# A hybrid decoder block on one core: the recurrence at 8.25 products a half instead of 8.5, gate loads behind operand loads, and another order of the first rows

## The chip, the cores and the metric

The kernel runs on one core of a Trainium2 chip. TensorE (PE) multiplies matrices into PSUM, VectorE (DVE) and ScalarE (ACT) do elementwise work, GpSimd (POOL) does small work and issues the transfers that add to memory, and SyncE (SP) issues most other transfers. Each of these takes its instructions in order, so an instruction that waits holds all that is queued behind it on its engine. The metric is the device time of one launch in microseconds (us), lower is better. The median of three runs before the change is 1466.38 us.

## The reference

One layer of a decoder block on x (1024 tokens x 1024 columns), float32:

```python
proj = x @ w_in                       # 1024 x 7168: q | f | i | o_gate | pool_v | gate_a | gate_b
qf = silu(q) * 128 ** -0.5
f = lb + (1 - lb) * sigmoid(f_pre); k = 1 - f
# 8 heads of 128: S_t = diag(f_t) S_{t-1} + k_t i_t^T,  o_t = S_t^T q_t
o = o * rsqrt(mean(o * o, per head) + RMS_EPS) * hgrn_norm_g * sigmoid(o_gate)
a = o @ w_a
pooled = causal_mean(pool_v, windows 2, 4, 8, 16 by group) - pool_v
b = (pooled, group by group, @ w_pool) * pool_scale
merged = sigmoid(gate_a) * a + sigmoid(gate_b) * b
x = layer_norm(2 ** 0.25 * x + merged @ w_out)
x = layer_norm(2 ** 0.25 * x + relu(x @ w_up) ** 2 @ w_down)
```

## The kernel before

**Products.** A float32 operand is split in a high part (a cast on ACT, L126 for weights, L131 for activations) and a low part (a subtract on DVE, L127 and L132). A product of a 512-row weight block with 512 tokens is 12 matmuls of 128x512: for each of four quarters of the contraction, high x high (L212), high x low (L214) and low x high (L215). The function `pair` computes four 512-token by 128-column blocks, each a sum of two such block products, with seven products instead of eight, in the manner of Strassen and Winograd: the weight blocks b11, b12, b21, b22 and their combinations T1 to T4 against the activation combinations a11, a12, a22, s1 to s4. An ordinary pair takes its operands in the order T0 (b11), b21, T2, T3, T1, T4, b22; a `twin` pair, in the w_a stage, in the order T0, b21, T3, T4, T2, T1, b22. T3 = b22 - b12 (L284) needs the last block loaded. Weight blocks live in a ring of six (`raw`), of which a pair takes five, so the loads of the next pair wait until combinations of this one have been split.

**Stages.** To about 97 us: x is transposed on PE (L170), split, and the value projection i is computed (L501 to L503). From 97 to 668 us: 24 pairs of w_in, for the heads' q and f (`head_inputs`), the output gates (`output_gates`), the pooled columns (`pooled`) and the gates a and b (`gates`). Then w_a in two runs of two pairs, w_out with the first norm, the MLP's up and down products, and the last norm at 1465.

**The recurrence** is a generator that runs beside the pairs of w_in: after each product PE takes one step of it (a "turn"). Its 16 halves (8 heads x 512 tokens) take `PER_HALF` = 8.5 products each, rounded; at a half's fourth turn the half before is put out (`turn_outputs`, L1034 multiplies by the output gate in the buffer `og`, and `put_output` stores it and adds it to up to three of the sums s1 to s4 in memory, by transfers on POOL, L640). The last half's output comes at turn 149, the second product of gates(6). ORDER is the list of pairs. Behind it come gates(6) and gates(7), with the 16 pooled products of w_pool (`pool_products`, L113 to L115) spread behind their products by `POOL_AFTER`. The weight parts of a pooled group lie in a ring of the tiles tD, tE, tF and og.

**Who sets the order.** From the first output gates to gates(7) PE's order is that of the code. On the other engines, a scheduler orders the instructions by priorities and estimated times; `issue_after` holds an instruction behind another.

**The w_a stage.** `o_operand` loads the recurrence's output and its sums (tiles c, L618) and splits them into a11, a12, s3, a22, s2, s1, s4, in this order, one ahead of each step. `gated` loads a gate a (tile ga) and the pooled result (tile gb) at the point at which a result block is ready, multiplies (L1120) and adds (L1121). The loads of both kinds are SP's.

Of the kernel before, what the change touches and what calls it, by code (L numbers as in the profile page):

```python
# [12 lines left out]
AF = mybir.ActivationFunctionType  # L13
# [13 lines left out]
HALO = 16  # L27
LINE = 16
NW = 10
PER_HALF = 8.5  # L30
TURN_BACK = 4
TURNS_AHEAD = 3
ORDER = (
    ("inputs", 1), ("pooled", 0), ("inputs", 2), ("gates", 0), ("output_gates", 2), ("inputs", 3), ("pooled", 1),
    ("inputs", 4), ("output_gates", 4), ("gates", 1), ("inputs", 5), ("pooled", 2), ("inputs", 6), ("output_gates", 6),
    ("gates", 2), ("inputs", 7), ("pooled", 3), ("gates", 3), ("gates", 4), ("gates", 5),
)
POOL_AFTER = {6: (1, 1, 1, 1, 1, 1, 2), 7: (2, 2, 2, 2, 0, 0, 0)}
PRIO_WHOLE = 6000
QUARTER = HALF // 2  # L40
PRIO = 60
# [10 lines left out]
def tile_hybrid_block(  # L52
# [18 lines left out]
    nc = tc.nc  # L71
# [83 lines left out]
    r = [None] * 8  # L155
    xp = {name: [None] * CH for name in ("a11", "a12", "a22", "s1", "s2", "s3", "s4")}

    made_last, made_hi = {}, {}

    @contextmanager  # L160
    def behind_parts(name):
# [10 lines left out]

    def in_parts(name, kp, src):
        xp[name][kp] = act_tile()
        made_last[name], made_hi[name] = (i.ins for i in split_into(xp[name][kp], src))


    xt = [[None] * CH for _ in range(3)]
# [88 lines left out]
    def pair(raw, rooms, takes, pz_tag="pj", twin=False, pc_tag="pj", turned=False):  # L267


        b11, b12, b21, b22, t = raw if len(raw) == 5 else (*raw, None)  # L270
        c, ps = {}, {}

        def copied(room, ps):
            t = room()
            A.copy(t, ps)  # L275
            return t

        def added(t, ps):
            V.tensor_add(t, t, ps)  # L279
            return t  # L280

        def make_t3():
            c["t"] = block_tile() if t is None else t
            V.tensor_sub(c["t"], b22, b12)  # L284

        def t3():
            if twin:
                make_t3()
            return w_part(c["t"])

        def t2():
            if not twin:
                make_t3()
                make_t2()
            return w_part(b11)

        def make_t2():
            if turned:
                minus_sum(b11, c["t"], b11)
            else:  # L300
                V.tensor_add(b11, c["t"], b11)

        def t4():
            if twin:
                make_t2()
            if turned:
                minus_sum(b21, b11, b21)
            else:
                V.tensor_sub(b21, b21, b11)
            return w_part(b21)  # L310

        def t1():
            if turned:
                minus_sum(b12, b22, b11)
            else:
                V.tensor_sub(b12, b22, b11)
            return w_part(b12)

        def p1(w):
            ps["a"] = ps_tile()  # L320
            prod(ps["a"], w, "a11", True)
            c[11] = copied(rooms[0], ps["a"])

        def p2(w):
            if pz_tag == "pj":
                ps["z"] = ps_tile()
# [97 lines left out]
    with tc.tile_pool(name="xr", bufs=8, side="right", reuse_waits="tile") as xr:  # L424
# [15 lines left out]
        V.tensor_max(lb, prm[:, 0:8], prm[:, 8:16])  # L440
        V.tensor_sub(e01[:, 0:8], prm[:, 0:8], lb)
        V.tensor_sub(e01[:, 8:16], prm[:, 8:16], lb)
        A.activation(e01, e01, AF.Exp)
        V.tensor_add(lb, e01[:, 0:8], e01[:, 8:16])
        V.reciprocal(lb, lb)
        V.tensor_mul(lb, lb, e01[:, 0:8])
        V.tensor_scalar(one_lb, lb, -1.0, 1.0, ALU.mult, ALU.add)
        g_neg = e01[:, 0:8]
        V.tensor_scalar_mul(g_neg, g_col, -1.0)
        x_rows = [xr.tile([P, CH, D], F32, name=f"x{u}", bufs=1) for u in range(2)]  # L450
        for t in range(8):
            r[t] = x_rows[t // CH][:, t % CH]
# [103 lines left out]
            put(0, 1, c, t)  # L556

        first_tokens("a11", "tr", "tr", "hg", "hg")
        w = parts(b11)
        first_tokens("a12", "tr")  # L560
        onto_chain(w, "a11", True, copied(c11, c_late))
        with behind_parts("a11"):
# [53 lines left out]
    def loaded(src, tile_of):  # L616
        t = tile_of()
        nc.sync.dma_start(out=t, in_=src)  # L618
        return t

    def o_operand(name):

        where = dict(a11=lambda kp: od[kp][0], a12=lambda kp: od[kp + CH][0], a22=lambda kp: od[kp + CH][1])
        for kp in range(CH):
            src = where[name](kp) if name in where else osd[name][kp]
            xp[name][kp] = act_tile()
            split_into(xp[name][kp], loaded(src, c_tile))
# [17 lines left out]
    with tc.tile_pool(name="tmp", bufs=1, side="right", reuse_waits="tile") as tmp:  # L645
# [470 lines left out]
        def gated(j, u, park):  # L1116

            def take(src):
                t = loaded(gad[j][u], mg_tile("ga", 12))
                V.tensor_mul(t, t, src)  # L1120
                V.tensor_add(t, t, loaded(pbd[j][u], mg_tile("gb", 2)))  # L1121
                if park:
                    parked[u, j] = t
                else:
                    merged[u][j] = split_act(t)
            return take
# [403 lines left out]
```

## Time and profile before

| | |
|---|---|
| median of 3 runs | 1466.38 us (1464.82 to 1467.86) |
| profiled execution | 1466.59 us |
| its span | 1464.9 us |
| around the span | 1.7 us |
| busy: PE / DVE / ACT / POOL | 1435.5 / 1100.1 / 759.0 / 107.6 us |
| 110 to 600 us (w_in pairs with the recurrence): PE busy | 484.0 of 490 us |
| 600 to 640 us (end of gates(5), gates(6)): PE busy, DMA share | 37.0 of 40 us, 0.87 |
| 640 to 668 us (gates(7)): PE busy, DMA share | 27.5 of 28 us, 0.84 |
| 668 to 720 us (first w_a pairs): PE busy, DMA share | 48.5 of 52 us, 0.73 |

The span is the profiled time from the first to the last recorded instruction. Busy time is a sum over one engine's instructions with overlaps counted once. In a row of a timeline stand the start, the duration, the engine, the line of the code, the operation, the tiles (written <- read) and the shape; what stands in brackets is the idle time of the engine before the instruction and what ended it. A "q" behind an engine's name is its queue of transfers: such a row shows the issue, not the transfer. PEclk, the granted clock, is the share of full speed at which PE may run in a stretch.

### The profile page before, as it was taken

The page shows a single profiled execution, that of the slowest core. Times are in us where ns is not written, and L with a number is a line of the kernel's source. Part 1 is how long each engine was busy: PE and PEld are TensorE (multiplying, and loading weights), DVE is VectorE, ACT ScalarE, POOL GpSimd, SP SyncE. Part 2 cuts the span into 40 slices and gives each one's busy share as a digit, 9 for nine tenths or more (in the row PEclk, how much of TensorE's full clock was granted, in tenths as well). Part 3 has the DMA queues.
Part 4 walks back from the last instruction along what each step waited for, and adds up shares of the span by engine and source line. Part 5 has one row for each costly group of instructions (what it writes and reads, how often), then busy time and mean ns, then how long its engine had stood idle before and what let it go on. Part 6 is the DMA issues. An engine that isn't in the chain of part 4 may idle for free.

```text
span 1464.9 us, 20840 instructions
## 1 busy us (share of the span) xinstructions
PE 1435.5 (98%) x7377; PEld 1188.4 (81%) x7377; DVE 1100.1 (75%) x1807; ACT 759.0 (52%) x1383; POOL 107.6 (7%) x288
## 2 busy tenths in 40 slices
PE   8999999999999999999999999999999999999997
PEld 7788888788878888877788878888888888888886
DVE  4967886796797796477985598666666787777977
ACT  5545566655755655555542366555556443333435
POOL 0002011211211210000002100000000100000000
PEclk9999999999999999999999999999999999999999
DMA  7142245345435546788673135444447774445422
GB/s 259 58 137 87 73 126 169 80 134 155 109 87 146 142 116 184 211 300 286 204 232 113 61 99 180 144 154 148 157 148 261 280 262 142 166 132 170 129 72 115
DMA packets 187161, 228.15 MB, mean 156 GB/s; under 512 B 12176, under 2 KB 110512, under 8 KB 187056
## 3 DMA queue, kind: packets, MB, share of 16 engines
q1 hardware_dynamic: 181088, 212.91, 43.9%
q0 software_dynamic: 5184, 11.54, 4.0%
q10 hardware_dynamic: 784, 2.38, 0.5%
q8 instruction: 58, 0.95, 0.3%
q14 instruction: 47, 0.39, 0.1%
HBM read 149.70 MB, written 77.07 MB: 155 GB/s over the span
## 4 chain that ended last, share of the span: by engine, by line
PE 87%; DVE 6%; DMA 4%; issue 1%; ACT 1%; SPq 0%; DVEq 0%; POOL 0%; ACTq 0%
PE ps_pj L212 15%; PE ps_pj L215 14%; PE ps_pj L214 14%; PE ps_pj L1412 4%; PE ps_pj L1413 4%; PE ps_pj L1411 4%; PE ps_pj L114 2%; PE ps_pj L113 2%; PE ps_pj L115 2%; PE ps_tr L1412 1%; PE ps_tr L1413 1%; PE ps_tr L1411 1%; PE ps_sc L215 1%; DVE w L127 1%; PE ps_hg L215 1%
## 5 line engine op out<-in xcount | busy, mean ns | idle before, releaser
L212 PE MATMUL ps_pj<-act,w 128*128 128x512 f32 x1068 | 420.2, 395 | 10.8 <-ACT c L275 3.3
L215 PE MATMUL ps_pj<-act,w 128*128 128x512 f32 x1068 | 415.7, 391 | 1.3 <-DVE w L127 1.3
L214 PE MATMUL ps_pj<-act,w 128*128 128x512 f32 x1068 | 415.0, 390 | 0.0
L126 ACT CAST w<-raw 128x512 fp32r<-128x512 f32 x310 | 192.5, 622 | 278.1 <-PE ps_pj L214 201.7
L127 DVE TENSOR_TENSOR w<-raw,w 128x512 fp32r<-128x512 f32 x310 | 212.1, 686 | 92.8 <-ACT w L126 87.6
L212 PEld LDWEIGHTS ps_pj<-act,w 128*128 128x128 f32 x1068 | 200.7, 188 | 56.9 <-ACT c L275 4.6
L215 PEld LDWEIGHTS ps_pj<-act,w 128*128 128x128 f32 x1068 | 200.8, 188 | 45.2 <-DVE w L127 2.6
L214 PEld LDWEIGHTS ps_pj<-act,w 128*128 128x128 f32 x1068 | 200.8, 188 | 40.8 <-DVE act L132 0.2
L1373 ACT CAST act<-act 128x1024 fp32r<-128x1024 f32 x66 | 66.9, 1050 | 109.0 <-issue 35.0
L279 DVE TENSOR_TENSOR c<-c,ps_pj 128x512 f32<-128x512 f32 x95 | 64.8, 682 | 39.1 <-PE ps_pj L215 35.6
L1374 DVE TENSOR_TENSOR act<-act,act 128x1024 fp32r<-128x1024 f32 x66 | 79.5, 1220 | 18.5 <-ACT act L1373 17.4
L1413 PE MATMUL ps_pj<-act,act 128*128 128x512 f32 x240 | 93.0, 389 | 0.0
L1412 PE MATMUL ps_pj<-act,act 128*128 128x512 f32 x240 | 93.0, 389 | 0.0
L1411 PE MATMUL ps_pj<-act,act 128*128 128x512 f32 x240 | 92.5, 389 | 0.0
L275 ACT COPY c<-ps_pj 128x512 f32<-128x512 f32 x96 | 55.8, 581 | 3.1 <-issue 1.8
L284 DVE TENSOR_TENSOR raw<-raw,raw 128x512 f32<-128x512 f32 x43 | 29.6, 690 | 33.2 <-DMA raw<-in_w_in_dram 28.8
L1411 PEld LDWEIGHTS ps_pj<-act,act 128*128 128x128 f32 x240 | 45.0, 188 | 9.4
L1412 PEld LDWEIGHTS ps_pj<-act,act 128*128 128x128 f32 x240 | 45.0, 188 | 9.4
L1413 PEld LDWEIGHTS ps_pj<-act,act 128*128 128x128 f32 x240 | 45.0, 188 | 9.3
L1282 ACT ACTIVATE c<-c 128x512 f32<-128x512 f32 x61 | 38.5, 632 | 1.7
L1281 ACT ACTIVATE c<-c 128x512 f32<-128x512 f32 x46 | 29.1, 632 | 15.0 <-DVE c L279 15.0
L1367 DVE TENSOR_TENSOR act<-act,ps_pj 128x512 f32<-128x512 f32 x45 | 30.1, 682 | 6.0 <-PE ps_pj L1413 5.7
(416 smaller groups left out, 2680.5 us busy)
## 6 DMA issues: line engine op xcount, KB each, us to landing
h<-c SPq DMA_DIRECT2D x106, 256.0 KB, 2.7
raw<-in_w_in_dram SPq DMA_DIRECT2D x100, 256.0 KB, 3.3
act<-h SPq DMA_DIRECT2D x78, 256.0 KB, 3.0
draw<-in_w_down_dram SPq DMA_DIRECT2D x16, 1024.0 KB, 7.6
raw<-in_w_up_dram SPq DMA_DIRECT2D x56, 256.0 KB, 2.8
hf<-h SPq DMA_DIRECT2D x34, 256.0 KB, 3.0
s<-og POOLq DMA_DIRECT2D x28, 256.0 KB, 6.1
v<-v SPq DMA_DIRECT2D x16, 256.0 KB, 3.3
```

The source lines that it names most:

```text
L126: A.copy(hi, src)
L127: V.tensor_sub(lo, src, f(hi))
L212: PE.matmul(ps, wh[:, k], th, start=first and k == 0, stop=False, skip_group_check=True)
L214: PE.matmul(ps, wh[:, k], tl, start=False, stop=False, skip_group_check=True)
L215: PE.matmul(ps, wl[:, k], th, start=False, stop=k == CH - 1, skip_group_check=True)
L275: A.copy(t, ps)
L279: V.tensor_add(t, t, ps)
L1373: A.copy(hi, src)
L1374: V.tensor_sub(lo, src, f(hi))
L1411: PE.matmul(ps, hh[:, w], wh, start=fresh and n == 0, stop=False, skip_group_check=True)
L1412: PE.matmul(ps, hh[:, w], wl, start=False, stop=False, skip_group_check=True)
L1413: PE.matmul(ps, hl[:, w], wh, start=False, stop=n == M - 1, skip_group_check=True)
```

## The change

- PER_HALF goes from 8.5 to 8.25. With the rounding, the 17 rounds take 140 products behind the first turns instead of 144, and the last half is put out at turn 145, the fifth product of gates(5), instead of turn 149.
- In ORDER inputs(7) stands ahead of gates(2).
- POOL_AFTER for gates(6) is (0, 1, 1, 1, 1, 2, 2) instead of (1, 1, 1, 1, 1, 1, 2): eight pooled products as before, the first one product later.
- In `pair` T2 is written over b12 instead of b11, and T1 into the tile t (that held T3) instead of b12. T4 is made from b12.
- At the start the third and fourth row of b11 are split behind the first tokens' second and fourth parts, and the small operations for lb and the norm gain stand behind the first tokens.
- In the w_a stage the loads of gate a and of the pooled result are held behind the last load of an operand issued so far in the code, and stand together. All three copies of a pair go into the ring `room`, now of 6; `ga` has 10 buffers instead of 12.

```diff
-PER_HALF = 8.5
+PER_HALF = 8.25
...
-    ("gates", 2), ("inputs", 7), ("pooled", 3), ("gates", 3), ("gates", 4), ("gates", 5),
+    ("inputs", 7), ("gates", 2), ("pooled", 3), ("gates", 3), ("gates", 4), ("gates", 5),
 )
-POOL_AFTER = {6: (1, 1, 1, 1, 1, 1, 2), 7: (2, 2, 2, 2, 0, 0, 0)}
+POOL_AFTER = {6: (0, 1, 1, 1, 1, 2, 2), 7: (2, 2, 2, 2, 0, 0, 0)}
...
-        made_last[name], made_hi[name] = (i.ins for i in split_into(xp[name][kp], src))
+        made_last[name], made_hi[name] = made_kp[name, kp] = [i.ins for i in split_into(xp[name][kp], src)]
...
-            return w_part(b11)
+            return w_part(b12)
 
         def make_t2():
             if turned:
-                minus_sum(b11, c["t"], b11)
+                minus_sum(b12, c["t"], b11)
             else:
-                V.tensor_add(b11, c["t"], b11)
+                V.tensor_add(b12, c["t"], b11)
...
-                V.tensor_sub(b21, b21, b11)
+                V.tensor_sub(b21, b21, b12)
...
-                V.tensor_sub(b12, b22, b11)
-            return w_part(b12)
+                V.tensor_sub(c["t"], b22, b12)
+            return w_part(c["t"])
...
-        w = parts(b11)
+        w = parts(b11[:2])
+        for row, kp in zip(b11[2:], (1, 3)):
+            lo_done, hi_done = made_kp["a11", kp]
+            with tc.issue_after(lo_done), tc.issue_after(hi_done):
+                w += parts([row])
+        with behind_parts("a11"):
+            V.tensor_max(lb, prm[:, 0:8], prm[:, 8:16])
...
+            split_into(xp[name][kp], t)
...
-                t = loaded(gad[j][u], mg_tile("ga", 12))
+                with tc.issue_after(last_load[0]):
+                    t = loaded(gad[j][u], mg_tile("ga", 10))
+                    more = loaded(pbd[j][u], mg_tile("gb", 2))
                 V.tensor_mul(t, t, src)
-                V.tensor_add(t, t, loaded(pbd[j][u], mg_tile("gb", 2)))
+                V.tensor_add(t, t, more)
...
-            room = mg_tile("room", 4)
+            room = mg_tile("room", 6)
...
-            return pair(raw, (c_tile, room, room), takes, "hg", True, turned=True)
+            return pair(raw, (room, room, room), takes, "hg", True, turned=True)
```

How this moves instructions is shown at three places. A row gives the line, the operation, the tile written <- the tiles read, and the shape.

ACT at the start, before: w are the high parts of the four rows of the weight block b, act those of the first tokens' four transposed parts (tiles ps).

```order
L126 CAST w_23_220<-b_2_154 128x512
L126 CAST w_25_224<-b_2_154 128x512
L126 CAST w_27_228<-b_2_154 128x512
L126 CAST w_29_232<-b_2_154 128x512
L443 ACTIVATE e01_138<-e01_138 128x16
L131 CAST act_16_189<-ps_tr_15_184 128x512
L131 CAST act_18_198<-ps_tr_17_193 128x512
L131 CAST act_20_207<-ps_sc_19_202 128x512
L131 CAST act_22_216<-ps_hg_21_211 128x512
```

The same place of ACT after the change; xt are plain copies of the transposed tokens:

```order
L126 CAST w_23_211<-b_2_145 128x512
L126 CAST w_25_215<-b_2_145 128x512
L131 CAST act_16_180<-ps_tr_15_175 128x512
L131 CAST act_18_189<-ps_tr_17_184 128x512
L131 CAST act_20_198<-ps_sc_19_193 128x512
L131 CAST act_22_207<-ps_hg_21_202 128x512
L126 CAST w_27_219<-b_2_145 128x512
L187 COPY xt0_141<-ps_tr_15_175 128x512
L187 COPY xt1_142<-ps_tr_17_184 128x512
L126 CAST w_29_223<-b_2_145 128x512
```

The four casts of tokens went from behind the third and fourth weight row and the exponential (L443) to ahead of them.

SP in gates(6), before: o7_1 is the last half's output being stored from the buffer og, pb are pooled results being stored, po and gb operands of pooled products, tC a block of w_pool, raw weight blocks of gates(7), c an operand of w_a.

```order
L636 DMA o7_1_918<-og_1198_6430 128x512
L727 DMA ga6_0_947<-c_1226_6540 128x512
L223 DMA raw_1292_6820<-in_w_in_dram 128x4x128
L783 DMA pb1_0_985<-f_1237_6587 128x512
L223 DMA raw_1294_6823<-in_w_in_dram 128x4x128
L618 DMA tH_1279_6780<-po4_1_976 128x512
L618 DMA c_1371_7134<-o5_0_913 128x512
L618 DMA tH_1280_6782<-po5_1_978 128x512
L618 DMA f_1270_6742<-gb3_0_957 128x512
L783 DMA pb0_1_984<-f_1248_6630 128x512
L223 DMA raw_1295_6825<-in_w_in_dram 128x4x128
L618 DMA tC_1263_6705<-in_w_pool_dram 128x2x256
```

The same place of SP after the change:

```order
L645 DMA o7_1_918<-og_1186_6351 128x512
L736 DMA gb5_1_962<-c_1199_6431 128x512
L223 DMA raw_1292_6820<-in_w_in_dram 128x4x128
L736 DMA ga5_1_946<-c_1196_6410 128x512
L736 DMA gb5_0_961<-c_1207_6499 128x512
L623 DMA tC_1265_6725<-in_w_pool_dram 128x2x256
L635 DMA c_1365_7119<-o2_0_907 128x512
L623 DMA st_1266_6727<-po4_0_975 128x512
L623 DMA st_1267_6729<-po5_0_977 128x512
L736 DMA ga6_0_947<-c_1227_6550 128x512
L792 DMA pb0_0_983<-f_1235_6576 128x512
```

The last output's store and the load of tC now stand ahead of every store of a pooled result; before, the store stood behind the first (pb0_0) and the load of tC behind the first three.

SP at the first w_a pairs, before: c are operands from the recurrence's output (o) and its sums (s1 to s4), ga and gb the gates and pooled results for `gated`.

```order
L618 DMA c_1420_7320<-s2_0_1003 128x512
L618 DMA ga_1412_7289<-ga0_0_935 128x512
L618 DMA ga_1416_7311<-ga2_0_939 128x512
L618 DMA ga_1444_7418<-ga0_1_936 128x512
L618 DMA ga_1447_7439<-ga2_1_940 128x512
L618 DMA c_1405_7260<-o7_1_918 128x512
L618 DMA ga_1461_7488<-ga1_1_938 128x512
L618 DMA ga_1463_7507<-ga3_1_942 128x512
L618 DMA c_1422_7325<-s2_1_1004 128x512
L618 DMA gb_1445_7421<-pb0_1_984 128x512
L618 DMA ga_1469_7533<-ga1_0_937 128x512
L618 DMA c_1424_7330<-s2_2_1005 128x512
```

The same place of SP after the change; raw are blocks of w_a, ga7 and pb7 gates being stored:

```order
L635 DMA c_1450_7446<-s4_0_1011 128x512
L736 DMA pb7_1_998<-q_1340_7005 128x512
L736 DMA ga7_1_950<-q_1329_6956 128x512
L223 DMA raw_1475_7561<-in_w_a_dram 128x4x128
L635 DMA c_1452_7451<-s4_1_1012 128x512
L736 DMA pb7_0_997<-og_1351_7084 128x512
L635 DMA c_1454_7456<-s4_2_1013 128x512
L635 DMA c_1456_7461<-s4_3_1014 128x512
L223 DMA raw_1476_7563<-in_w_a_dram 128x4x128
L623 DMA ga_1412_7289<-ga0_0_935 128x512
L623 DMA ga_1416_7311<-ga2_0_939 128x512
L623 DMA ga_1444_7418<-ga0_1_936 128x512
```

All operand loads, the last of s4 with them, now stand ahead of the first gate load.

More of the change, by code (lines that the diff above doesn't have):

```diff
@@ L156, in tile_hybrid_block @@
     xp = {name: [None] * CH for name in ("a11", "a12", "a22", "s1", "s2", "s3", "s4")}
-    made_last, made_hi = {}, {}
+    made_last, made_hi, made_kp = {}, {}, {}
     @contextmanager
@@ L306, in t4 @@
             if turned:
-                minus_sum(b21, b11, b21)
+                minus_sum(b21, b12, b21)
             else:
-                V.tensor_sub(b21, b21, b11)
+                V.tensor_sub(b21, b21, b12)
             return w_part(b21)
@@ L313, in t1 @@
             if turned:
-                minus_sum(b12, b22, b11)
+                minus_sum(c["t"], b22, b12)
             else:
-                V.tensor_sub(b12, b22, b11)
-            return w_part(b12)
+                V.tensor_sub(c["t"], b22, b12)
+            return w_part(c["t"])
         def p1(w):
@@ L439, in tile_hybrid_block @@
         e01 = const.tile([P, 16], F32, name="e01")
[L440 to L449, printed above, removed]
         x_rows = [xr.tile([P, CH, D], F32, name=f"x{u}", bufs=1) for u in range(2)]
@@ L558, in tile_hybrid_block @@
         first_tokens("a11", "tr", "tr", "hg", "hg")
-        w = parts(b11)
+        w = parts(b11[:2])
[5 more added lines that the diff above has]
+            V.tensor_max(lb, prm[:, 0:8], prm[:, 8:16])
+            V.tensor_sub(e01[:, 0:8], prm[:, 0:8], lb)
+            V.tensor_sub(e01[:, 8:16], prm[:, 8:16], lb)
+            A.activation(e01, e01, AF.Exp)
+            V.tensor_add(lb, e01[:, 0:8], e01[:, 8:16])
+            V.reciprocal(lb, lb)
+            V.tensor_mul(lb, lb, e01[:, 0:8])
+            V.tensor_scalar(one_lb, lb, -1.0, 1.0, ALU.mult, ALU.add)
+            g_neg = e01[:, 0:8]
+            V.tensor_scalar_mul(g_neg, g_col, -1.0)
         first_tokens("a12", "tr")
@@ L619, in loaded @@
         return t
+    last_load = [None]
     def o_operand(name):
@@ L626, in o_operand @@
             xp[name][kp] = act_tile()
-            split_into(xp[name][kp], loaded(src, c_tile))
+            t = c_tile()
+            last_load[0] = nc.sync.dma_start(out=t, in_=src).ins
+            split_into(xp[name][kp], t)
     FIRST = {(0, 0): ("s3", "s2", "s4"), (0, 1): ("s1",), (1, 0): (), (1, 1): ()}
```

## The prediction

> **What bounds the kernel.** I read the share of each engine first, then the chain that ended last, then what TensorE (PE) waited for, and last the places of these waits in the timeline.
>
> ```profile
> PE 1435.5 (98%) x7377; PEld 1188.4 (81%) x7377; DVE 1100.1 (75%) x1807; ACT 759.0 (52%) x1383; POOL 107.6 (7%) x288
> PE 87%; DVE 6%; DMA 4%; issue 1%; ACT 1%; SPq 0%; DVEq 0%; POOL 0%; ACTq 0%
> PE ps_pj L212 <- ACT w L126: 2.7, 2, 2.2
> PE ps_hg L212 <- ACT act L131: 2.1, 1, 2.1
> PE ps_pj L501 <- ACT act L131: 2.0, 1, 2.0
> PE ps_pj L215 <- DVE w L127: 1.3, 3, 0.7
> PE ps_pj L212 <- ACT room L275: 1.0, 1, 1.0
> ```
>
> PE is busy for 98% of the span and is 87% of the last chain. The number and shape of its products don't change, so the edit can win only where PE stands idle (1464.9 - 1435.5 = 29.4 us, beginning and end included) or runs at half clock. The last five rows are waits (total, times, longest) at three places that the change touches: the start, the pooled products in gates(6), and the w_a stage.
>
> **What an idle stretch costs besides its own length.** A row of the next view: stretch, its length, then busy time of PE, PEld, DVE, ACT, POOL, granted clock, DMA share, GB/s.
>
> ```profile
> 9.70:13.10 3.40, 1.38 (x10) 1.05 (x8) 1.94 (x6) 2.50 (x6) 0.00 (x0) 1.00 1.05 405
> 13.10:16.50 3.40, 3.40 (x10) 2.65 (x9) 2.90 (x9) 3.40 (x8) 0.00 (x0) 0.50 1.05 387
> 627.50:630.90 3.40, 1.33 (x5) 0.80 (x6) 3.40 (x7) 2.80 (x5) 0.00 (x0) 1.00 0.97 324
> 630.90:634.30 3.40, 3.40 (x10) 2.63 (x9) 1.21 (x2) 0.24 (x1) 0.00 (x0) 0.50 1.05 339
> 685.50:688.90 3.40, 1.63 (x8) 0.98 (x6) 2.75 (x5) 0.31 (x1) 0.00 (x0) 1.00 0.94 294
> 688.90:692.30 3.40, 3.01 (x12) 2.18 (x13) 1.99 (x3) 1.94 (x4) 0.00 (x0) 1.00 0.99 365
> ```
>
> A stretch of 3.4 us with PE busy for 1.38 or 1.33 is followed by 3.4 us at clock 0.50; after one with 1.63 the clock stays at 1.00. What a half-clock stretch costs shows in the spacing of matmuls of the same shape, at 13 us and at 637 us:
>
> ```profile
> 13.67 0.63 PE L501 MATMUL ps_pj<-w,act 128*128 128x512 f32 x1
> 14.10 0.63 PE L502 MATMUL ps_pj<-w,act 128*128 128x512 f32 x1
> 637.09 0.39 PE L212 MATMUL ps_pj<-act,w 128*128 128x512 f32 x1
> 637.32 0.39 PE L214 MATMUL ps_pj<-act,w 128*128 128x512 f32 x1
> ```
>
> They start 0.43 us apart instead of 0.23. So 3.4 us hold 8 matmuls that full clock does in 8 x 0.23 = 1.8 us: 1.6 us lost each time. A product of 12 matmuls takes 12 x 0.227 = 2.7 us.
>
> [...]
>
> **Part 1, the start: -3.6 us.**
>
> ```profile
> 7.87 0.62 ACT L126 CAST w<-b 128x512 fp32r<-128x512 f32 x1 [1.82 <-DMA b<-in_w_in_dram]
> 10.60 1.14 ACT L126 CAST w<-b 128x512 fp32r<-128x512 f32 x2 [2.12 <-DMA b<-in_w_in_dram]
> 11.64 0.21 ACT L443 ACTIVATE e<-e 128x16 f32<-128x16 f32 x1
> 11.76 1.05 ACT L131 CAST act<-ps_tr 128x512 fp32r<-128x512 f32 x2
> 9.76 0.60 PE L170 MATMUL ps_hg<-ident,x 128*128 128x128 f32 x4
> 12.38 0.50 PE L501 MATMUL ps_pj<-w,act 128*128 128x512 f32 x1 [2.02 <-ACT act L131]
> ```
>
> ScalarE (ACT) has the second row of weights cast at 8.49, then stands 2.12 us at the third row, whose load isn't in; the cast of the first tokens (L131) that PE waits for is queued behind it, behind the fourth row's and behind the small exponential. The change puts the four token casts ahead of these three. The first then starts at about 8.5, the high half is there at 9.1 and the low half, one DVE subtract of about 0.7 later, near 9.8; PE itself is at its last transposes until 10.36. So the first product starts at about 10.4 instead of 12.38: -2.0. With PE busy from there, 9.7 to 13.1 no longer is a stretch with 1.38, and the half-clock stretch behind it goes: -1.6. The two late weight rows are cast from about 11, and PE comes to the third after two quarters of the product, 10.4 + 2 x 2.7 = 15.8, so they are covered; so are the lower-bound operations, which the first head needs much later. Bounds: -3.9, if the casts also come closer together by the 0.2 of the exponential, and -2.0, if a half-clock stretch forms anyway. I take -3.6, since 3.3 of these 3.4 us would be busy.
>
> **Part 2, the last half of the recurrence and the pooled products: -3.5 us.**
>
> ```profile
> 610.00 2.62 POOL L640 DMA_DIRECT2D s<-og  x3 [25.82 <-DVE og L1034]
> 620.52 0.69 DVE L127 TENSOR_TENSOR og<-tC,tF 128x512 fp32r<-128x512 f32 x1 [2.31 <-DMA s<-og]
> 622.30 0.67 SPq L618 DMA_DIRECT2D tC<-in_w_pool_dram  x1
> 627.71 0.62 ACT L126 CAST tD<-tC 128x512 fp32r<-128x512 f32 x1 [3.37 <-DMA tC<-in_w_pool_dram]
> 628.90 0.50 PE L212 MATMUL ps_pj<-act,w 128*128 128x512 f32 x1 [2.16 <-ACT w L126]
> 630.30 0.50 PE L215 MATMUL ps_pj<-act,w 128*128 128x512 f32 x1 [0.67 <-DVE w L127]
> ```
>
> The last head's output is gated just before 610 and added to the stored sums by three POOL transfers; its buffer is wanted for the low half of a pooled weight block (og<-tC,tF at 620.52), which waits for them. Only then is tC free, its load goes at 622.30, and ACT stands at its cast until 627.71 with the next gate weight's cast queued behind: PE waits 2.16, then 0.67, and falls to half clock for 1.6. All together 4.4. At 8.25 products a half the last output comes four products earlier (turn 145 instead of 149, 4 x 2.7 = 11 us), while the pooled products start one later; buffer and load come free before they are wanted. I keep back 0.9, since the last two products of gates(6) now have two pooled products each and ask ACT and DVE for operands as closely as here, where a late split cost PE 0.67. Bounds: -4.4, and +2.2, if one wait like the 2.16 arises behind those doubled products and nothing is won.
>
> **Part 3, the w_a stage: -2.0 us.**
>
> ```profile
> 682.01 1.27 SPq L618 DMA_DIRECT2D ga<-ga  x3
> 683.23 0.69 DVE L1120 TENSOR_TENSOR ga<-ga,c 128x512 f32<-128x512 f32 x1 [0.62 <-DMA ga<-ga]
> 688.59 1.14 ACT L131 CAST act<-c 128x512 fp32r<-128x512 f32 x2 [3.36 <-DMA c<-o]
> 689.26 0.49 PE L212 MATMUL ps_hg<-act,w 128*128 128x512 f32 x1 [2.13 <-ACT act L131]
> 699.71 0.50 PE L212 MATMUL ps_pj<-act,w 128*128 128x512 f32 x1 [0.99 <-ACT room L275]
> ```
>
> SP issues gate loads (ga) among the operand loads (c) of the recurrence's output; an operand lands late, ACT waits 3.36 and PE 2.13, later 0.99. The change puts all operand loads ahead of all gate loads, with two more rooms for the copies. Removable: 3.1 and two waits below 0.3 that I count as 0.4: 3.5. The gate loads are late now: DVE's multiply by a gate, already 0.62 late, holds the weight splits queued behind it. I charge two such waits, 1.2, and 0.3 for the gb ring of two, whose loads SP now issues with the ga loads: -2.0. Bounds: -3.5, and +3.4, if what ACT waits here (3.36) DVE waits for a gate, with PE behind it. No half-clock stretch is won, as the 1.00 in the rows above shows.
>
> **Part 4, the recurrence itself: 0.** Between 110 and 600 us:
>
> ```profile
> 110.00:600.00 490.00, 484.00 (x3155) 405.31 (x3154) 386.37 (x785) 292.61 (x650) 83.36 (x236) 1.00 0.45 125
> DVE raw L284 <- DMA raw<-in_w_in_dram: 28.8, 16, 4.5
> 280.79 0.69 DVE L284 TENSOR_TENSOR raw<-raw,raw 128x512 f32<-128x512 f32 x1 [3.46 <-DMA raw<-in_w_in_dram]
> 289.36 0.50 PE L212 MATMUL ps_pj<-act,w 128*128 128x512 f32 x1 [1.62 <-ACT c L275]
> SPq L618 <- DMA s<-og: 50.1, 15, 7.6
> ```
>
> PE loses 490 - 484 = 6.0 us. DVE waits 28.8 us, in 16 places, for the block b22 that T3 needs; one of these, 3.46 at 280.79, is followed by a PE wait of 1.62 at 289.36. SP is the cause: it stands 50.1 us at loads of output gates that wait for POOL's adding transfers, and the weight loads stand behind. Putting T2 over b12 frees b21's place two products earlier, but b22 still waits for the split of T1 (the tile is another, the moment the same). Making the turns 3% denser (8.25 for 8.5) brings each head's transfers closer to weight loads in some pairs and away from them in others; DVE is at 386/490 = 79% and would go to about 81%. ORDER swaps inputs(7) and gates(2), with the same products. I take 0 between -6.0 (all idle time gone) and +22.8 (all 28.8 reaches PE instead of 6.0): nearest to the row of before.
>
> **Sum.** -3.6 - 3.5 - 2.0 + 0 = -9.1. The profiled execution took 1466.6 (span 1464.9 and 1.7 around it), 0.2 above the median of the runs: 1457.5.
>
> **Rivals.**
> A, the recurrence gains too (chance 0.17): with other distances, og loads miss the adding transfers and five of the 6.0 us go: 1452.5. For it: only 5 of the 16 DVE waits reach PE, so small shifts decide. Against: the denser turns.
> B, only the start comes (0.17): the operand and pooled-weight loads move into stretches such as 627.5 to 634.3, where the DMA share is 0.97 and 1.05 already, and land no sooner in effect, so that parts 2 and 3 come to nothing: 1466.6 - 3.6 = 1463.0. Against it: the waits there were for transfers issued late, at 622.30 and 682.01 and after.
> [...]
> D, slower (0.19): the T3 waits. One mechanism, in the pairs from inputs(1) to gates(5): SP blocked at an og load, b22 late, DVE late, and with less slack in denser turns PE pays. It decides when PE loses 6.0 + 9.1 = 15.1 of 28.8; two thirds of it, 19.5, give 1471, which I take as its time; all 28.8 give 1480.3. For it: DVE has little room to catch up in denser turns. Against: today 11 of the 16 waits cost PE nothing.
>
> **Chances.** The case of the sum has 0.40, with 1454 to 1461 as its own range. No change within 0.2% is 2.9 us, about the spread of the three runs. Faster: the sum, A and C, and half of B, which lies at the bound: 0.72. Same: half of B and 0.05 of D: 0.14. Slower: the rest of D, 0.14. The range 1451 to 1467 leaves out some 0.05 below (the far end of A) and D's 0.14 above.
>
> **What would show it.** The first product at 10.4 and clock 1.00 from 13.1; no PE wait near 627 and the tC load ahead of the pooled stores; no ACT wait for c<-o behind 680, and DVE waits for ga below 1 us each. The prediction falls if PE's waits between 110 and 600 come to more than some 10 us, or if DVE's waits for ga or gb stop PE in w_a.

## The result

The changed kernel takes 1459.84 us (median of 5 runs, 1454.56 to 1460.58) against 1466.32 us (median of 5, 1464.82 to 1467.86): a ratio of 0.9948, 95% interval 0.9934 to 0.9962, so 5.6 to 9.7 us faster. 1457.5 was forecast, with a range of 1451 to 1467. The profiled execution of the changed kernel took 1460.42 us with a span of 1458.7, 6.2 below the span before.

The total is close to the forecast, but its terms are not, and the largest errors cancel. What PE waits for in the whole span shows it (page of waits, PE, after; total, times, longest):

```profile
PE ps_pj L212 <- ACT c L275: 5.6, 3, 3.1
PE ps_pj L212 <- ACT w L126: 5.3, 1, 5.3
PE ps_hg L433 <- POOL inv_n L149: 1.7, 1, 1.7
PE ps_sc L170 <- DMA x<-in_x_dram: 0.9, 1, 0.9
PE ps_pj L212 <- ACT f L275: 0.8, 1, 0.8
```

The waits for the first tokens (2.0), for the w_a operands (2.1) and for `room` (1.0) are gone. In their place stands one wait of 5.3 for a weight's cast, longer than any before.

To place gains and losses I take the start of the same matmul in both timelines: the first of the first w_in pair, of gates(4), of gates(7), of w_a and of the second two w_a pairs. Before:

```profile
97.52 0.39 PE L212 MATMUL ps_pj<-act,w 128*128 128x512 f32 x1
556.38 0.39 PE L212 MATMUL ps_pj<-act,w 128*128 128x512 f32 x1
637.09 0.39 PE L212 MATMUL ps_pj<-act,w 128*128 128x512 f32 x1
668.17 0.39 PE L212 MATMUL ps_pj<-act,w 128*128 128x512 f32 x1
710.72 0.39 PE L212 MATMUL ps_pj<-act,w 128*128 128x512 f32 x1
```

After:

```profile
92.86 0.39 PE L212 MATMUL ps_pj<-act,w 128*128 128x512 f32 x1
553.11 0.50 PE L212 MATMUL ps_pj<-act,w 128*128 128x512 f32 x1
630.57 0.39 PE L212 MATMUL ps_pj<-act,w 128*128 128x512 f32 x1
668.83 0.39 PE L212 MATMUL ps_pj<-act,w 128*128 128x512 f32 x1
706.91 0.39 PE L212 MATMUL ps_pj<-act,w 128*128 128x512 f32 x1
```

Differences of neighbours place the gains and losses. The last but one column is explained below the table.

| stretch | before, us | after, us | difference | for the same work | forecast |
|---|---|---|---|---|---|
| start to the first w_in pair | 97.52 | 92.86 | -4.7 | -4.7 | -3.6 |
| w_in pairs up to gates(4) | 458.86 | 460.25 | +1.4 | -2.3 | 0 |
| gates(4) to the end of gates(7) | 111.79 | 115.72 | +3.9 | +7.6 | -3.5 |
| first two w_a pairs | 42.55 | 38.08 | -4.5 | -4.5 | -2.0 |
| from there to the end | 754.18 | 751.79 | -2.4 | -2.4 | 0 |
| sum | | | -6.2 | -6.2 | -9.1 |

The second and third row do not compare the same work. With the denser turns, matmuls of the recurrence that stood behind the first product of gates(4) stand ahead of it (windows of the second row; before, then after):

```profile
97.52:556.38 458.86, 452.86 (x2947) 379.01 (x2946) 368.34 (x747) 274.51 (x604) 80.15 (x233) 1.00 0.42 119
```

```profile
92.86:553.11 460.25, 456.52 (x3020) 381.78 (x3018) 371.30 (x758) 277.44 (x614) 81.63 (x235) 1.00 0.44 121
```

These are 73 matmuls and, at the same clock, 3.7 us of PE's time (456.52 - 452.86). Taken out of the second row and put back into the third, they leave -2.3, which is the idle time of PE that went (6.0 to 3.7), and +7.6.

**The start** went as forecast (timeline, ACT and PE, and the windows; after):

```profile
7.42 0.58 ACT L131 CAST act<-ps_tr 128x512 fp32r<-128x512 f32 x1 [0.22 <-PE ps_tr L170]
9.89 0.47 PE L491 MATMUL ps_pj<-w,act 128*128 128x512 f32 x1
9.70:13.10 3.40, 3.40 (x19) 2.85 (x17) 2.37 (x7) 3.36 (x7) 0.00 (x0) 1.00 1.05 400
13.10:16.50 3.40, 3.40 (x18) 2.76 (x17) 2.27 (x9) 2.57 (x6) 0.00 (x0) 1.00 1.05 391
```

The tokens' cast stands at 7.42, the first product starts at 9.89 (12.38 before), and the clock is 1.00 where it was 0.50.

**From gates(4) to gates(7)** two new waits appear. The first is at 559 (timeline, SP, ACT, then PE; after):

```profile
555.82 0.45 SPq L623 DMA_DIRECT2D tC<-in_w_pool_dram  x1
560.33 0.62 ACT L126 CAST tD<-tC 128x512 fp32r<-128x512 f32 x1 [4.20 <-DMA tC<-in_w_pool_dram]
560.85 0.61 ACT L126 CAST w<-raw 128x512 fp32r<-128x512 f32 x1
562.00 0.50 PE L212 MATMUL ps_pj<-act,w 128*128 128x512 f32 x1 [3.14 <-ACT c L275]
```

The recurrence now ends four products sooner, so the tile tC is free sooner, the first pooled weights are loaded at 555.82, and ACT has their cast in its queue at once. It stands there for 4.20 us until the load is in, with a weight cast and the copy that frees PE's PSUM bank queued behind it. The pooled products that need these weights come some 45 us later.

The second is at 636 (same views):

```profile
635.50 0.73 SPq L635 DMA_DIRECT2D c<-o  x1
640.46 0.62 ACT L131 CAST act<-c 128x512 fp32r<-128x512 f32 x1 [7.80 <-DMA c<-o]
640.98 0.61 ACT L126 CAST w<-raw 128x512 fp32r<-128x512 f32 x1
641.65 0.80 PE L212 MATMUL ps_pj<-act,w 128*128 128x512 f32 x1 [5.27 <-ACT w L126]
640.80:644.20 3.40, 2.55 (x6) 1.96 (x7) 3.06 (x5) 2.32 (x5) 0.00 (x0) 0.60 1.04 370
```

ACT stands 7.80 us at the cast of the first w_a operand, which is needed at 668, and the weight for gates(7)'s second product is queued behind it. The wait at 627 that the change was forecast to remove is gone, and gates(7) starts 6.5 us earlier than before, at 630.57. But the operand's load, on SP behind the pooled operands and stores, is issued at 635.50, where before it was issued at 634.34: PE arrives earlier at something that does not come earlier. A clock of 0.60 goes with it.

ACT's order is not new here. Before the change the same cast stood ahead of the same weight's cast (timeline, ACT, before):

```profile
639.93 0.62 ACT L131 CAST act<-c 128x512 fp32r<-128x512 f32 x1 [1.73 <-DMA c<-o]
640.45 0.62 ACT L126 CAST w<-raw 128x512 fp32r<-128x512 f32 x1
```

It waited 1.73 us, and PE, which came later, waited for nothing. So the loss sits in gates(7), which takes 38.26 us instead of 31.08 for the same products. From gates(4) to gates(6) the change comes out nearly even: PE is idle for 3.0 us before and 3.3 after, with the wait at 559 in place of the one at 627.

**The w_a stage** has no wait left (windows of 668 to 725; first before, then after):

```profile
668.00:725.00 57.00, 53.48 (x231) 42.66 (x230) 48.03 (x78) 29.98 (x54) 0.00 (x0) 1.00 0.72 238
```

```profile
668.00:725.00 57.00, 57.00 (x253) 47.22 (x252) 49.56 (x81) 28.31 (x51) 0.00 (x0) 1.00 0.67 222
```

### The profile page after: what moved, and what is told of

It reads as the page before. It is cut to its first block, busy times and chain, and to the rows that moved or that the text cites. A ratio compares the mean times of both kernels' runs of the same rounds, so it can differ in the third digit from the quotient of the medians.

```text
span 1458.7 us, 20882 instructions
## 1 busy us (share of the span) xinstructions
PE 1433.3 (98%) x7377; PEld 1188.7 (81%) x7377; DVE 1100.4 (75%) x1807; ACT 759.3 (52%) x1383; POOL 106.7 (7%) x288
## 4 chain that ended last, share of the span: by engine, by line
PE 86%; DVE 7%; DMA 3%; ACT 2%; issue 1%; SPq 0%; DVEq 0%; ACTq 0%
PE ps_pj L212 14%; PE ps_pj L215 14%; PE ps_pj L214 14%; PE ps_pj L1423 4%; PE ps_pj L1424 4%; PE ps_pj L1422 4%; PE ps_pj L114 2%; PE ps_pj L115 2%; PE ps_pj L113 2%; PE ps_tr L1423 1%; PE ps_tr L1424 1%; PE ps_tr L1422 1%; DVE w L127 1%; PE ps_hg L212 1%; PE ps_sc L215 1%
```

## The experiments

Twelve runs were made, in three groups of four. A group shares its chip and its runs of the kernel before (medians 1467.36, 1466.21 and 1465.92 us). Times of the same kernel spread over several us, so the ratio to before and its interval carry the verdicts; "PE idle" is a window's length less PE's busy time in it, in one profiled execution.

| run | kernel | median us | ratio, 95% interval |
|---|---|---|---|
| e1 | start alone | 1461.57 | 0.9964 (0.9951 to 0.9977) |
| e2 | w_a alone | 1461.09 | 0.9962 (0.9950 to 0.9974) |
| e3 | turns alone | 1471.89 | 1.0027 (1.0013 to 1.0041) |
| e4 | all but the turns | 1458.07 | 0.9939 (0.9926 to 0.9952) |
| e5 | the change again | 1461.78 | 0.9969 (0.9953 to 0.9985) |
| e6 | change, operand casts held | 1459.51 | 0.9949 (0.9932 to 0.9966) |
| e7 | change, both casts held | 1454.98 | 0.9920 (0.9907 to 0.9933) |
| e8 | T2 over b12 alone | 1467.92 | 1.0006 (0.9994 to 1.0017) |
| e9 | start and w_a | 1456.24 | 0.9930 (0.9916 to 0.9945) |
| e10 | e7 with POOL_AFTER as before | 1461.23 | 0.9961 (0.9947 to 0.9974) |
| e11 | change, rooms as before | 1466.42 | 1.0005 (0.9993 to 1.0017) |
| e12 | e7 with T2 over b11 | 1456.21 | 0.9928 (0.9911 to 0.9945) |

### e1: the start alone

```diff
-        w = parts(b11)
+        w = parts(b11[:2])
+        for row, kp in zip(b11[2:], (1, 3)):
+            lo_done, hi_done = made_kp["a11", kp]
+            with tc.issue_after(lo_done), tc.issue_after(hi_done):
+                w += parts([row])
+        with behind_parts("a11"):
+            V.tensor_max(lb, prm[:, 0:8], prm[:, 8:16])
...
```

> The kernel before with the edits of the start alone. Theory (the gain at the start is real and stands by itself): 3.6 to 4.7 us faster than before, first product near 10 us, clock 1.00 from 13.1 to 16.5 us, and the stages behind it wait as before (6.0 us between 110 and 600, 2.2 and 0.7 near 627, 2.1 and 1.0 near 689 and 699). Rival (an earlier start is given back at a later wait): less than 2 us faster.

Measured 0.36% or 5.3 us faster (3.4 to 7.2). The waits behind stand where they stood, some of them smaller in this execution (1.39 near 283, 1.41 near 622, 0.97 and 1.23 in w_a). The gain is real and stands by itself, and the forecast of 3.6 lies in its interval.

### e2: the w_a edits alone

```diff
-                t = loaded(gad[j][u], mg_tile("ga", 12))
+                with tc.issue_after(last_load[0]):
+                    t = loaded(gad[j][u], mg_tile("ga", 10))
+                    more = loaded(pbd[j][u], mg_tile("gb", 2))
...
-            room = mg_tile("room", 4)
+            room = mg_tile("room", 6)
...
-            return pair(raw, (c_tile, room, room), takes, "hg", True, turned=True)
+            return pair(raw, (room, room, room), takes, "hg", True, turned=True)
```

> The kernel before with the w_a edits alone. Theory (operands ahead of gates take away all of PE's waits there): PE without a wait above 0.1 us from 668 to 720, 4.5 to 5 us faster. My term of the prediction: 2.0 faster, with DVE waits for ga. Rival for the 2 us that the changed kernel won near 865 and 875: if they come from the w_a edits they show here too (6.5 to 7 us faster in all).

Measured 5.6 us faster (3.8 to 7.3). PE is busy for the whole of 668 to 725 in this run too. Near 865 to 876 one wait of 0.64 is left of three (0.21, 0.53, 0.84): part of what the changed kernel won in the MLP belongs to these edits. A wait of 1.04 for `room` near 739 is new here and absent in the changed kernel.

### e3: PER_HALF, ORDER and POOL_AFTER alone

```diff
-PER_HALF = 8.5
+PER_HALF = 8.25
...
-POOL_AFTER = {6: (1, 1, 1, 1, 1, 1, 2), 7: (2, 2, 2, 2, 0, 0, 0)}
+POOL_AFTER = {6: (0, 1, 1, 1, 1, 2, 2), 7: (2, 2, 2, 2, 0, 0, 0)}
```

> The kernel before with PER_HALF, ORDER and POOL_AFTER alone (T2 over b11 as before). Prediction's term: 3.5 us faster. Theory now (pool weights and the first w_a operand are asked for earlier than their transfers can bring them, ACT stands in order, PE waits near 559 and 636): 3 to 6 us slower than before, with PE waits of 2 us or more at both places, and half clock behind the second. Rival (the added waits of the changed kernel come from T2 over b12 instead): same as before or faster.

Measured 4.0 us slower (1.9 to 6.0): the term of -3.5 has the wrong sign. The waits are those of the changed kernel without its T2 (timeline, PE, e3):

```profile
568.77 0.50 PE L212 MATMUL ps_pj<-act,w 128*128 128x512 f32 x1 [1.54 <-ACT c L275]
646.37 0.80 PE L212 MATMUL ps_pj<-act,w 128*128 128x512 f32 x1 [5.39 <-ACT w L126]
```

The first is shorter than forecast, 1.54. Between 110 and 525 us PE idle is 8.2 us instead of 6.0: the denser turns cost in the recurrence too.

The start of this run is as before, with a PE wait of 1.96 for the first tokens (2.02 before). Even so no half-clock stretch stands behind it (windows, e3):

```profile
9.70:13.10 3.40, 1.44 (x10) 1.07 (x9) 1.94 (x6) 2.58 (x6) 0.00 (x0) 1.00 1.05 404
13.10:16.50 3.40, 3.40 (x16) 2.81 (x15) 2.82 (x9) 3.40 (x8) 0.00 (x0) 1.00 1.05 389
```

The first w_in pair starts at 95.82, 1.7 us earlier than before, without an edit at the start.

### e4: all but the turns

```diff
-PER_HALF = 8.25
+PER_HALF = 8.5
```

and ORDER and POOL_AFTER as before.

> The changed kernel with PER_HALF, ORDER and POOL_AFTER as before, so with the start, T2 over b12 and w_a edits. Theory (the turns give back 5 us): 1453 to 1456, 4 to 7 us faster than the changed kernel, PE waits near 627 as before (2.2 and 0.7). Rival (the prediction: the turns win 3.5): 1462 to 1464.

Measured 0.9939, against 0.9948 for the changed kernel, the intervals overlapping: the time alone doesn't show the 5 us that the theory gave to the turns. Nor were the waits near 627 as before. DVE's low half of the pooled weights in `og` waits longer for POOL's adding transfers than before (2.31 then), and it reaches PE at once, 2.60 instead of 2.16, with a smaller one of 1.08 near 635 (timeline, DVE and PE, e4):

```profile
613.17 0.69 DVE L127 TENSOR_TENSOR og<-tC,tF 128x512 fp32r<-128x512 f32 x1 [4.34 <-DMA s<-og]
614.52 0.80 PE L215 MATMUL ps_pj<-act,w 128*128 128x512 f32 x1 [2.60 <-DVE w L127]
```

So the old hand-over still costs, as the prediction had it; the denser turns do remove PE's wait there, and put their own in its place. DVE's wait they don't remove: in the changed kernel it is 6.05, ahead of 607.23, and PE waits for nothing behind it. The profiled execution took 1454.02 us, the lowest of this kernel's five, so its profile shows its good side.

### e5: the changed kernel again

No edit; the base for e6 and e7 on their chip.

> The changed kernel unchanged, as the base for the runs beside it. 6 to 8 us faster than before; PE waits of about 3 near 559 and 5 near 636 if these belong to the order of the instructions, elsewhere or absent if they were an accident of one execution.

4.5 us faster than before (2.2 to 6.9), less than the 6 to 8 expected. The waits are at the same two places, 2.95 near 563 and 5.46 near 641, so they belong to the order of the instructions; others (2.27 near 503) came and went between the two executions.

### e6: the first w_a operand's casts held on ACT

```diff
+    w_casts = []
     def w_part(src):
-        return split(src, w_tile)
+        hi, lo = w_tile(), w_tile()
+        w_casts.append(A.copy(hi, src).ins)
+        V.tensor_sub(lo, src, f(hi))
+        return hi, lo
...
-        o_operand("a11")
+        with tc.issue_after(w_casts[-7:][3]):
+            o_operand("a11")
```

> The changed kernel with the eight casts of the first w_a operand (a11) held on ACT behind gates(7)'s cast for T3 instead of in front of its second weight cast. Theory (ACT stands at a cast whose load is not in, with PE's weight cast queued behind): the wait of 5.3 near 636 goes and with it the half clock behind, 5 to 6.5 us faster than the changed kernel, the wait near 559 stays. Rival (SP and the transfers are late, not ACT's order): PE waits 3 us or more there for another load, at most 2 us faster.

Measured 0.9949 against 0.9969 beside it: 2 to 3 us faster by the medians, not the 5 to 6.5 of the theory, and not clear of noise. The wait for the weight's cast is gone, and another stands there (timeline, DVE and PE, e6):

```profile
642.34 0.75 DVE L796 SCALAR_TENSOR_TENSOR f<-ps_tr,prm,f 128x512 f32<-128x512 f32 x1 [3.51 <-DMA f<-gb]
643.14 0.50 PE L113 MATMUL ps_tr<-w,tD 128*128 128x512 f32 x1 [2.42 <-DVE f L796]
```

A pooled result waits 3.51 for its gate b, whose load SP issues late, and PE 2.42 for the PSUM bank. Both readings hold a part: ACT's order made some 5.3 into a wait, and SP's lateness takes back 2.4 and the half clock (0.56 in the stretch from 644).

### e7: both casts held

```diff
-            pl = parts(*todo[0], *soon.pop(0))
+            with tc.issue_after(w_casts[-8]):
+                pl = parts(*todo[0], *soon.pop(0))
```

> As the run before, and ACT's casts of the first pooled weight group held behind gates(4)'s last weight cast. Theory: the wait of 3.1 near 559 goes too, 2.5 to 3.5 us faster than with the first hold alone, 1450 to 1453 in all. Rival (a later wait for the pooled operands takes its place): no faster than with the first hold alone.

Measured 1454.98, a ratio of 0.9920: the intervals of e5 and e7 don't touch, those of e6 and e7 meet only at 0.9932 to 0.9933. The 1450 to 1453 us expected were missed by 2. Between 525 and 600 us the profile has (windows; e5, then e7):

```profile
525.00:600.00 75.00, 72.05 (x450) 60.30 (x449) 50.93 (x106) 42.94 (x97) 6.45 (x15) 0.98 0.52 151
```

```profile
525.00:600.00 75.00, 74.72 (x468) 62.63 (x467) 53.46 (x110) 44.76 (x100) 9.09 (x18) 1.00 0.60 170
```

2.95 us of waiting become 0.28 and the clock stays at 1.00. This shows the mechanism at 559: a cast that nothing needed for 45 us stood ahead of one that PE needed. The wait for a gate b near 637, new in e6, is still there (PE 2.86). With the two holds the kernel beats the kernel before and the changed one.

### e8: T2 over b12 alone

```diff
-            return w_part(b11)
+            return w_part(b12)
...
-                V.tensor_add(b11, c["t"], b11)
+                V.tensor_add(b12, c["t"], b11)
```

> The kernel before with T2 over b12 (and T1 over t) alone. Prediction's reading: no effect, since b22's load waits for the split of T1 in both. Reading from the traces so far (with the start and w_a edits the waits of PE between 100 and 525 fell by 2.1 us): 1.5 to 2.5 us faster, with less than 4.5 us of PE waits between 110 and 600 instead of 6.0.

The time is that of before (0.9994 to 1.0017), but not because nothing happens. Between 110 and 525 us DVE waits less for b22 (waits of DVE; before, then e8):

```profile
DVE raw L284 <- DMA raw<-in_w_in_dram: 23.2, 14, 3.5
```

```profile
DVE raw L284 <- DMA raw<-in_w_in_dram: 19.0, 13, 2.7
```

and PE idle there falls from 6.0 to 3.9 us. The 1.5 to 2.5 us expected don't come, since PE idle from 600 to 668 rises from 3.5 to 5.5. The longest wait there is new (timeline, PE, e8):

```profile
619.26 0.50 PE L215 MATMUL ps_pj<-act,w 128*128 128x512 f32 x1 [3.10 <-DVE w L127]
```

The weight's split (DVE, 618.52) is queued behind the low half of the pooled weights in `og` (617.91), which waits 2.78 for POOL's adding transfers: the place and cause of the 2.60 in e4.

### e9: the start and the w_a edits together

The edits of e1 and e2.

> The kernel before with the start and the w_a edits together, recurrence, pooled products and T2 as before. Theory (the two gains add, the rest of the change gives back what T2 wins): 5.3 + 5.6 = 10.9 us faster than before, about 1455.5, with PE waits as before between 110 and 660. Rival (they share a gain, an earlier start or a later stage eats one): 6 to 8 us faster, no better than the changed kernel.

0.9930, 10.3 us faster (8.1 to 12.3): the two gains add (5.3 + 5.6). These two edits alone are at least as good as the whole change.

### e10: e7 with POOL_AFTER as before

```diff
-POOL_AFTER = {6: (0, 1, 1, 1, 1, 2, 2), 7: (2, 2, 2, 2, 0, 0, 0)}
+POOL_AFTER = {6: (1, 1, 1, 1, 1, 1, 2), 7: (2, 2, 2, 2, 0, 0, 0)}
```

> The changed kernel with both holds on ACT and POOL_AFTER for gates(6) as before, so the first pooled product behind the first product. Theory of the prediction's 0.9 (two pooled products behind each of gates(6)'s last products ask for more than SP brings): the wait of 2.9 near 637 (a pooled result waiting for its gb load) shrinks below 1 and the kernel is 1 to 3 us faster than with the holds alone. Rival (SP's chain of stores and loads sets the rate of pooled products wherever they start): the same wait there or an earlier one, time within 1 us.

Slower: 0.9961 against 0.9920 for e7 (another chip, the intervals apart). The wait near 637 does go, and three earlier ones come: 1.41 near 609, 2.67 near 627, 1.15 near 630. So starting the pooled products one product later is worth having once the turns are denser, as far as runs on two chips can tell; my reading that it takes something back was wrong, and the rival is the nearer one.

### e11: the changed kernel with the rooms as before

```diff
-            room = mg_tile("room", 6)
+            room = mg_tile("room", 4)
...
-            return pair(raw, (room, room, room), takes, "hg", True, turned=True)
+            return pair(raw, (c_tile, room, room), takes, "hg", True, turned=True)
```

> The changed kernel with the rooms of a w_a pair as before (the first copy in the ring of c, four in the ring of rooms). If the order of the loads alone carries the w_a gain: no PE wait from 668 to 720, same time. If the rooms carry the part near 700 (PE 0.99 waiting for a copy before) or the part near 865 to 876: waits of 1 us and of 2 us come back there, 1 to 3 us slower than the changed kernel.

The whole gain of the change is lost, more than the 1 to 3 us expected: 1.0005. The w_a stage waits again (windows; timeline, SP and PE; e11):

```profile
668.00:725.00 57.00, 53.62 (x229) 43.46 (x228) 49.05 (x81) 30.73 (x56) 0.00 (x0) 0.97 0.74 243
676.36 2.72 SPq L635 DMA_DIRECT2D c<-o  x3
686.54 0.73 PE L212 MATMUL ps_pj<-act,w 128*128 128x512 f32 x2 [2.87 <-ACT act L131]
```

Holding the gate loads is still in this kernel; without the rooms PE is idle for 3.4 us in this stretch, about as long as before (3.5), and the gate loads stand among the operand loads again (from 682.20 to 694.03). What it takes is another place for the first copy of a pair; whether that alone would do, without the hold, was not run. In the ring of c it takes buffers that the operands are loaded into, and SP issues three blocks of the fourth operand (a22) only at 676.36; with the copies in their own ring the changed kernel issues three of the same operand at 653.61 (timeline, SP, after):

```profile
653.61 1.53 SPq L635 DMA_DIRECT2D c<-o  x3
```

Two of the three waits of the MLP (0.21 and 0.83 near 864 and 874) come back as well.

### e12: e7 with T2 over b11

The edit of e8 undone in e7.

> The changed kernel with both holds and T2 over b11 as before. Reading from the run with T2 over b12 alone (PE waits between 100 and 525 down by 2.6, a new wait of 3 near 616): in the denser recurrence T2 over b12 wins 2 to 4 us between 100 and 525, so this is 2 to 4 us slower than with the holds alone. Rival (T2's place matters only by shifting transfers by chance): within 1 us or faster.

0.9928 against 0.9920: no difference that the intervals show. In the profile T2's place is seen all the same, PE idle between 110 and 525 us is 8.8 us (5.2 in e7), while from 600 to 668 it is 3.6 (3.9). The expected 2 to 4 us are there in that stretch, and the total doesn't follow it. The profiled execution took 1459.28, the longest of this kernel's six, so its profile shows its bad side.

## Why the prediction was right, and where it was not

**The total** came out near because errors cancel: two terms were undersized, by 1.1 and 2.5 us, the stages behind the first w_a pairs won 2.4 and the recurrence 2.3 that were not forecast; against this stand 11.1 us in one term with the wrong sign. That these nearly cancel is luck.

**Part 1, the start (-3.6; -4.7 in the profile, 5.3 in e1).** The step holds: the cast was moved out from behind the late rows, the first product started 2.5 us earlier (2.0 forecast) and the half-clock stretch of 1.6 went. That stretch does not come every time: of the four profiled executions with the old start three have it (before, e2, e8) and one has none (e3); of the ten with the new start none has it. Of the rest, part is the wait for x, 0.9 instead of 1.3, which differed from execution to execution (0.5 to 2.3) and is no effect of the edit.

**Part 2 (-3.5; +7.6 for the same work).** The failed step is "buffer and load come free before they are wanted". The load does: the one of 622.30 goes at 607.95, ACT's cast of it at 619.39 waits for nothing, and PE's waits of 2.16 and 0.67 went. The buffer does not: DVE waits longer for it than before (6.05 instead of 2.31), but PE does not. And I asked only what comes free and not what is met earlier as a consequence. The first pooled weights' cast goes to an earlier place of ACT's queue, in front of casts that PE needs in gates(4). The operand's cast keeps its place in front of gates(7)'s second weight, but PE gets there 6.5 us sooner, while SP delivers the operand no sooner. I had taken the orders of SP for gates(6) as evidence and not read ACT's at the same places. e3 shows the sign; e7 shows the first cast as a cause, and e6 the second, with SP's late loads as the other half. The 0.9 kept back for the doubled pooled products was aimed at the wrong edit (e10).

**Part 3 (-2.0; -4.5 there, e2 -5.6).** The waits went as worked out, 3.5 us, and the charge of 1.5 for late gates did not come: DVE has no wait for ga or gb left from 668 to 725, and PE waits for nothing behind the three for gb that follow (the longest 1.83, at 729.90). But the mechanism was named wrong. The order of the loads on SP was read as the effect of holding the gates; e11 shows that it does not come without the rooms, which I counted as an aside. The 2.4 us further on were priced at nothing; e2 and e11 tie a part of them to the w_a edits (PE idle from 860 to 880 is 1.58 before, 0.64 in e2, 0.22 after, 1.05 in e11), but which instruction order in the MLP carries them was not traced.

**Part 4 (0; -2.3 for the same work).** The other execution of the changed kernel (e5) has 0.4 more PE idle than before instead of 2.3 less, so zero is not refuted. It is made of two effects: T2 over b12 wins about 2 us there (e8: PE idle 6.0 to 3.9, DVE's waits for b22 down from 23.2 to 19.0), although b22's load waits for the split of T1 in both, as the step said; that the loads ahead of it on SP leave sooner would explain it, but was not traced; and the denser turns cost about 2 (e3 has 8.2 for 6.0; e12, with the old T2 as well, 8.8 for the 6.8 of e9).

**The rivals.** A did not come: PE idle in 110 to 525 us fell by 2.3 in one execution of the changed kernel (3.7) and rose by 0.4 in the other (6.4). B had it the wrong way round: the w_a gain came whole. C (0.07: the half-clock stretches have another cause than PE's idle time and stay, 1466.6 - 2.0 - 1.9 - 2.0 = 1460.7) is not borne out: at the start the half clock is seen only in executions with the idle stretch, and no run shows another cause. The stretches of 3.4 us ahead of the two half-clock ones before had PE busy for 1.38 and 1.33. The prediction's 1.63 is no border: in e8 the 3.4 us ahead of two half-clock stretches, from 640.86 and from 698.88 (mean clock 0.95 from 600 to 668 and 0.97 from 668 to 725), had PE busy for 1.83 and 1.71, and in e3 a stretch with 1.44 had none behind it. How much idle time it takes stays open. D named the right part of the change, but not the main mechanism: the turns do cost, but DVE's waits for b22 hardly changed (23.2 to 24.9 between 110 and 525, 26.2 in e5), and the larger cost sits behind ACT's casts. In one place of e5 D's chain may be seen: DVE waits 7.07 for b22 ahead of 493.95 (4.16 in the other execution), and PE 2.27 for DVE near 503.

**What stays open:** how much the turns cost beside T2 over b12. Alone they are 4.0 us slower (e3); with the rest of the change, e4 and the changed kernel differ by 0.0009 in ratio, within noise. The old turns bring the wait near 627, or with T2 over b12 the one for the adding transfers near 612; the new ones bring those near 559 and 636. With both holds (e7, e12) neither is left, and a pooled result waits for its gate b instead. ORDER was never changed apart from PER_HALF, so its share of the turns' cost is not known. Which of the three kernels e7, e9 and e12 is the best can't be told either: their intervals overlap, and they ran on two chips.

## What to carry to other kernels

- When a buffer comes free earlier, look up where each in-order engine now meets the work that this sets free: a cast whose load is in flight, standing ahead of one that the bottleneck needs, turned 11 us of earliness into 8.4 us of waiting. Hold such work behind the urgent instruction of the same engine (e7).
- A long-lived result in the ring that loads are made into held up the loads queued behind it: three blocks of a22 were issued at 676.36 instead of 653.61 us. Without a ring of its own for it the w_a stage kept nothing of its gain (e11: PE idle for 3.4 us from 668 to 725, 3.5 before).
- Check a sum term by term. This one was off by 2.9 us against the profile in total and by 11.1 us in a single term. When stretches of two kernels are compared, count the instructions in each first: a reordering moves work across their borders.

## What was not expected of the hardware

- Runs of the changed kernel spread further (1454.56 to 1460.58; in e5 1456.96 to 1467.33) than runs of the kernel before beside them (1464.82 to 1467.86; 1463.79 to 1470.47). The cause is not shown. The two profiled executions of the changed kernel differ for one in DVE's wait for a transfer ahead of 494 (7.07 and 4.16), with 2.27 of PE's waiting behind the longer one and none behind the other.
- A longer idle time did not cost more clock: behind PE's wait of 5.27 us the matmuls start 0.43 us apart for 3.2 us (641.65 to 644.80, clock 0.50), about as long as behind the wait of 2.16 before (630.90 to 634.30, clock 0.50). But the cost is not always one stretch: in e10, behind waits of 2.67 and 1.15, the clock is 0.50 from 630.16 to 636.98, twice as long.
